# Eight products instead of seven in the first chunks of each feed-forward, with the combined inputs formed beside them

## The chip, the cores and the metric

The kernel runs on one core of one Trainium2 chip. The metric is the device time of one execution in microseconds (us). The engines are named as the profile names them: PE (TensorE; its weight loads are PEld), DVE (VectorE), ACT (ScalarE), POOL (GpSimd) and SP (SyncE, which only issues DMAs here).

## What is computed

One step of one hybrid decoder layer on 1024 prompt tokens and 64 sample tokens (1088 columns together), float32, model width 1024, feed-forward width 2816. The change touches only the two feed-forward parts, which stand before and after the mixing part:

```python
h = x + 0.5 * _swiglu(_rmsnorm(x, w['ffn1_norm']), w['ffn1_w1'], w['ffn1_w3'], w['ffn1_w2'])
...          # projection, windowed attention, recurrent heads, gates, w_out
y = h + 0.5 * _swiglu(_rmsnorm(h, w['ffn2_norm']), w['ffn2_w1'], w['ffn2_w3'], w['ffn2_w2'])

def _rmsnorm(x, g):
    y = xf * lax.rsqrt(jnp.mean(xf * xf, axis=-1, keepdims=True) + EPS)
    return y * g
def _swiglu(x, w1, w3, w2):
    return (jax.nn.silu(x @ w1) * (x @ w3)) @ w2
```

## The kernel before, in words

The residual stands transposed in SBUF: eight tiles `h[k]` of 128 features by 1088 tokens. Every float32 matrix product is made of three fp32r matmuls: each operand is split into a high part (ACT casts it to fp32r: `split`, L137) and a low part (the difference, on DVE or POOL: L138), and the products high·high, high·low and low·high are added in PSUM.

A feed-forward has two stages. **Stage A** (`stage_a`) makes silu(u·w1) times u·w3, where u is the normed residual, for 22 chunks of 128 of the 2816 features, and stores each chunk to DRAM (`p_d`). The second stage multiplies by w2. Stage A takes w1 and w3 of a chunk, the two halves of the 1024 input features and two pairs of token quarters (272 tokens each) as a 2x2 block product. That would be eight block products; the kernel computes seven (Strassen-Winograd, the table `PRODUCTS`). A block product is four matmul triples for each of two token groups `s`, so 24 matmuls of 272 columns, and a chunk has 168 of them. The weights are combined per chunk on POOL (`sums13`, L427) and split by `parts13`. The inputs are combined once per feed-forward, in `combine(s, kb, ...)` for s = 0, 1 and kb = 0 to 3:

- two POOL multiplications of 544 columns (h times the reciprocal root mean square, L303) and two DVE multiplications by the gain (L304) give the four normed quarters `q`;
- four DVE operations of 272 columns make the combinations `tt` (L306 to L309);
- two splits give seven slots of high and low parts, `U[s,"h"]` and `U[s,"l"]` (tiles u0h, u0l, u1h, u1l): ACT casts of 816 and 1088 columns, a POOL difference of 816 and a DVE difference of 1088.

In the first chunk the products run with s = 0 alone and then with s = 1 alone; all others take both. `combine(1, ...)` is deferred into that first chunk.

Ahead of the first feed-forward, `load_x` loads nine token tiles, squares them on ACT, transposes them on PE (L275), copies them into `h` (L278), takes the root (`rstd`, L216 to L222), spreads it over the partitions with matmuls (`spread`, L287 to L289) and calls `combine`, for tiles 0 to 4 and then for 5 to 8. Ahead of the second, the last product of the mixing part (`flush` over four ranges of 272 columns) updates `h` on DVE (L575), `norm_half(g, s, k)` squares `h` (L382, L385), sums on PE (L389) and calls `combine` for s = 0 after the second range and for s = 1 after the fourth.

The Python program sets the order of emission: functions are put off by `defer` against a clock of PE time and run from `tick` between matmuls, or by `force` at the latest. The framework's scheduler then orders each engine's queue, and every engine runs its queue strictly in order. Wait points are semaphores. PSUM has eight banks; in the first part of a stage they are handed out singly (`psum`), from `banks(False)` on in three pairs (`pair`).

Of the kernel before, what the change touches and what calls it, by code (L numbers as in the profile page):

```python
# [58 lines left out]
class Layer:  # L59
    def __init__(self, tc, ctx, io):  # L60
# [165 lines left out]
    def load_x(self, g, weights):  # L226
# [35 lines left out]
        group(rest)  # L262
        rb = self.spread([(0, 96, dgs[4][:, 32:P])] + [(96 + j * P, P, dgs[5 + j]) for j in range(3)]
                         + [(480, 32, dgs[8][:NS, 0:32]), (512, 32, dgs[8][:NS, 32:NS])])
        self.close("xl")
        self.open("ar", "right", "u1h", "u1l")
        for kb in range(4):
            self.defer(1.0 + 2.2 * kb, lambda kb=kb: self.combine(1, kb, g, rb), ("u", 1))

    def h_part(self, i, x, m, half):  # L270
# [1 line left out]
        ph = self.psum((P, 4, P))
        for c in range(4):
            k = half * 4 + c
            nc.tensor.transpose(ph[:, c, :m], x[:m, k * P:(k + 1) * P], self.ident[:m, :m])  # L275
        for c in range(4):
            k = half * 4 + c
            (nc.scalar.copy if half else nc.vector.tensor_copy)(out=self.h[k][:, i * P:i * P + m], in_=ph[:, c, :m])  # L278
# [1136 lines left out]
```

## Time and profile before

| | |
|---|---|
| median of 3 runs | 2487.96 us (2485.41 to 2488.25) |
| profiled execution | 2485.03 us, its span in the trace 2483.2 us |
| busy | PE 95%, DVE 55%, ACT 28%, POOL 18% |
| chain that ended last | PE 89%, DVE 6%, DMA 2%, ACT, POOL and issue 1% each |
| matmuls of stage A (L487) | 36% of that chain |

PE is busy nearly everywhere. The slices of the page in which it isn't are the first two of 40 and the 28th and 29th (62 us each): the start of the first feed-forward and the start of the second. A busy share is not a speed: the row PEclk is the clock that was granted to PE, and it is low in the same slices.

### The profile page before, as it was taken

The numbers are of one execution on the slowest core, as the hardware profiler recorded it, in microseconds if no ns is written. First come the engines' busy times: TensorE is split into PE (matmuls) and PEld (weight loads), VectorE is DVE, ScalarE is ACT, GpSimd is POOL, SyncE is SP. The second block draws the span as 40 slices with busy tenths as digits, with TensorE's granted clock in tenths as the row PEclk, the third lists the DMA queues.
The fourth block names the chain that finished last, engine by engine and source line by source line (L and its number), as shares of the span: only waits on it lengthen the run. The fifth ranks groups of instructions, "written<-read, shape, count | busy, mean of one in ns | idle before, by whom it ended". The sixth has DMA issues, their size and how long they took to land.

```text
span 2483.2 us, 40296 instructions
## 1 busy us (share of the span) xinstructions
PE 2363.5 (95%) x16635; PEld 2330.5 (94%) x16635; DVE 1354.3 (55%) x2348; ACT 703.8 (28%) x1299; POOL 443.3 (18%) x321
## 2 busy tenths in 40 slices
PE   2699999999999999999999999995899999999999
PEld 2699999999999899999999999994799999999999
DVE  6744444457676724440544447658644444467766
ACT  4322222232121523332222254323222222231211
POOL 4522222210000411111111100026322222200000
PEclk6799999999999999999999999996899999999999
DMA  3122222234233222112112285300122222242312
GB/s 107 58 80 74 73 76 74 75 119 162 74 106 74 84 72 68 56 62 77 48 56 67 81 265 162 94 4 11 58 79 79 79 79 79 79 143 103 105 38 73
DMA packets 226468, 207.97 MB, mean 84 GB/s; under 512 B 22835, under 2 KB 207956, under 8 KB 226268
## 3 DMA queue, kind: packets, MB, share of 16 engines
q1 hardware_dynamic: 215168, 195.79, 25.3%
q10 hardware_dynamic: 11116, 9.60, 1.2%
q8 instruction: 131, 2.15, 0.4%
q14 instruction: 53, 0.43, 0.1%
HBM read 152.20 MB, written 54.13 MB: 83 GB/s over the span
## 4 chain that ended last, share of the span: by engine, by line
PE 89%; DVE 6%; DMA 2%; ACT 1%; POOL 1%; issue 1%; ACTq 0%; SPq 0%; DVEq 0%; POOLq 0%
PE pp L487 36%; PE ps L199 15%; PE ps L201 15%; PE ps L200 15%; PE ps L1062 2%; PE ps L871 1%; DVE q L304 1%; PE ps L836 1%; DVE tt L308 1%; DVE tt L306 1%; DMA raw<-in_ffn_w 1%; PE ps L861 1%; DMA g<-gate_d 1%; DVE tt L307 0%; POOL q L303 0%
## 5 line engine op out<-in xcount | busy, mean ns | idle before, releaser
L575 DVE SCALAR_TENSOR_TENSOR h<-ps,h 128x384 f32<-128x384 f32 (+2 forms) x632 | 326.3, 529 | 192.8 <-PE ps L201 192.5
L487 PE MATMUL pp<-u1h,wah 128*128 128x272 f32 x1232 | 359.3, 293 | 21.4 <-ACT u1h L137 17.6
L487 PE MATMUL pp<-u1l,wah 128*128 128x272 f32 x1232 | 357.5, 290 | 15.7 <-POOL u1l L138 15.7
L487 PE MATMUL pp<-u0h,wah 128*128 128x272 f32 x1232 | 360.4, 292 | 2.9 <-DVE ep L492 1.3
L487 PE MATMUL pp<-u1h,wal 128*128 128x272 f32 x1232 | 358.6, 291 | 3.4 <-DVE wal L138 3.4
L487 PE MATMUL pp<-u0h,wal 128*128 128x272 f32 x1232 | 361.2, 293 | 0.0
L487 PE MATMUL pp<-u0l,wah 128*128 128x272 f32 x1232 | 360.1, 292 | 0.0
L199 PE MATMUL ps<-ph,wbh 128*128 128x384 f32 (+1 forms) x1056 | 346.3, 328 | 0.3 <-DVE ev L492 0.3
L201 PE MATMUL ps<-ph,wbl 128*128 128x384 f32 (+1 forms) x1056 | 344.9, 327 | 0.0
L200 PE MATMUL ps<-pl,wbh 128*128 128x384 f32 (+1 forms) x1056 | 344.7, 326 | 0.0
L199 PE MATMUL ps<-u,wah 128*128 128x384 f32 (+1 forms) x768 | 259.3, 338 | 0.0
L487 PEld LDWEIGHTS pp<-u1h,wah 128*128 128x128 f32 x1232 | 234.2, 191 | 24.4 <-ACT u1h L137 19.7
L201 PE MATMUL ps<-u,wal 128*128 128x384 f32 (+1 forms) x768 | 251.3, 327 | 0.0
L487 PEld LDWEIGHTS pp<-u1l,wah 128*128 128x128 f32 x1232 | 235.1, 191 | 17.2 <-POOL u1l L138 17.2
L200 PE MATMUL ps<-u,wah 128*128 128x384 f32 (+1 forms) x768 | 251.1, 327 | 0.0
L487 PEld LDWEIGHTS pp<-u0h,wah 128*128 128x128 f32 x1232 | 236.3, 192 | 4.3 <-DVE ep L492 2.4
L487 PEld LDWEIGHTS pp<-u1h,wal 128*128 128x128 f32 x1232 | 235.2, 191 | 4.1 <-DVE wal L138 4.1
L487 PEld LDWEIGHTS pp<-u0l,wah 128*128 128x128 f32 x1232 | 236.4, 192 | 0.0
L487 PEld LDWEIGHTS pp<-u0h,wal 128*128 128x128 f32 x1232 | 236.0, 192 | 0.0
L137 ACT CAST wah<-raw 128x1024 fp32r<-128x1024 f32 x134 | 140.8, 1050 | 272.7 <-issue 98.8
L137 ACT CAST wah<-sm 128x1024 fp32r<-128x1024 f32 x96 | 80.2, 835 | 447.2 <-PE pp L487 441.1
L199 PEld LDWEIGHTS ps<-ph,wbh 128*128 128x128 f32 x1056 | 198.8, 188 | 1.1 <-DVE ev L492 0.6
(324 smaller groups left out, 4318.4 us busy)
## 6 DMA issues: line engine op xcount, KB each, us to landing
raw<-in_ffn_w SPq DMA_DIRECT2D x132, 512.0 KB
pl<-p_d SPq DMA_DIRECT2D x44, 544.0 KB
p_d<-ep SPq DMA_DIRECT2D x80, 272.0 KB
raw<-in_w_in SPq DMA_DIRECT2D x34, 512.0 KB
gate_d<-gt SPq DMA_DIRECT2D x40, 192.0 KB
g<-gate_d SPq DMA_DIRECT2D x32, 192.0 KB
h_d<-h ACTq DMA_DIRECT2D x8, 544.0 KB
h<-h_d SPq DMA_DIRECT2D x8, 544.0 KB
```

The lines of the kernel that those rows point to most:

```text
L137: nc.scalar.copy(out=hi, in_=src)
L199: nc.tensor.matmul(out, lhsT=wh, rhs=uh, start=(i == 0), stop=False)
L200: nc.tensor.matmul(out, lhsT=wh, rhs=ul, start=False, stop=False)
L201: nc.tensor.matmul(out, lhsT=wl, rhs=uh, start=False, stop=(i == n - 1))
L304: nc.vector.tensor_scalar(out=q[:, 2 * j:2 * j + 2, :], in0=q[:, 2 * j:2 * j + 2, :], scalar1=g[:, k:k + 1], scalar2=None, op0=ALU.mult)
L306: nc.vector.tensor_tensor(out=tt[:, 1, :], in0=q[:, 2, :], in1=q[:, 0, :], op=ALU.subtract)
L308: nc.vector.tensor_tensor(out=tt[:, 2, :], in0=q[:, 1, :], in1=tt[:, 1, :], op=ALU.add)
L487: nc.tensor.matmul(out, lhsT=w[:, kw], rhs=u[:, slot, kb, :], start=(opens and kb == 0 and j == 0), stop=(kb == 3 and j == 2), skip_group_ ...
L575: nc.vector.scalar_tensor_tensor(out=self.h[k][:, sl], in0=po[:, :n], scalar=scale, in1=self.h[k][:, sl], op0=ALU.mult, op1=ALU.add)
L836: nc.tensor.matmul(pq[kv][:, i, :w], lhsT=self.q[c][hs, q0:q0 + P], rhs=self.kT[hs, k0:k0 + w], start=True, stop=True)
L861: nc.tensor.transpose(pp[:, c, :], sts[kv][0][:, c, j * P:(j + 1) * P], self.ident)
L1062: nc.tensor.matmul(pl[:, c], lhsT=ke[:, c, :], rhs=qv[:, c, :, 1, :], start=True, stop=True)
```

## The change

- The first three chunks of the first feed-forward and the first two of the second (`np_` = 3 and 2) are computed by a new function `plain` with eight products. They need only the four normed quarters, not the combinations. In chunk 0 the products go kb by kb, so that kb = 0 can start alone; in later plain chunks all of w1 comes before w3.
- The norm is `normed`: two DVE operations of 544 columns (`scalar_tensor_tensor`, h times gain times reciprocal root) in place of two on POOL and two on DVE. `quarters` splits the four quarters at once (ACT cast and DVE difference of 1088 columns each); POOL has no part in it.
- The combinations come later, in eight calls of `three` (4.0 us of PE time apart, from `mixed`), which norm again and form and split three slots; `fourth` forms the last one for all kb at once from the high and low parts, after the plain chunks. The slot numbers in `PRODUCTS` are renamed to match.
- Chunk 0 needs no `sums13`, and its weights are split once instead of twice over. Only chunk 0's weights are loaded before tiles 5 to 8.
- `load_x`: squares and transposes of tiles 5 to 8 are deferred into chunk 0; `h_part` transposes two tiles into one PSUM bank and copies 256 columns at a time, DVE one feature block of the bank and ACT the other.

The core of the diff:

```diff
+        ss = squares(range(0, 5))
+        for i in (0, 2, 4):
+            for k in range(0, KC, 2):
+                self.h_part(xt[i:i + 2] if i < 4 else xt[4:5], i * P, k)
+        diagonals(range(0, 5), ss)
         rb = self.spread([(i * P, P, dgs[i]) for i in range(4)] + [(512, 32, dgs[4][:, 0:32])])
         for kb in range(4):
-            self.combine(0, kb, g, rb)
...
+            self.quarters(0, kb, g, rb)
...
+        self.defer(1.0, rest, ("u", 1))
+        self.defer(4.5, norm, ("u", 1))
...
+    def normed(self, s, kb, g, rb):
...
+        for j in range(2):
+            k = kb + 4 * j
+            nc.vector.scalar_tensor_tensor(out=q[:, 2 * j:2 * j + 2, :].rearrange("p a n -> p (a n)"), in0=self.h[k][:, c0:c0 + 2 * QN], scalar=g[:, k:k + 1],
+                                           in1=rb[:, 0:2 * QN], op0=ALU.mult, op1=ALU.mult)
...
+        self.split(self.U[s, "h"][:, 0:4, kb, :], self.U[s, "l"][:, 0:4, kb, :], self.normed(s, kb, g, rb))
...
+            self.defer(2.0 + 4.0 * i, lambda s=s, kb=kb: self.three(s, kb, g, rbs[s]), "t")
+
+    def three(self, s, kb, g, rb):
+        nc = self.nc
+        q = self.normed(s, kb, g, rb)
         tt = self.t("e", [P, 4, QN], F32, 3, name="tt")
...
-            nc.gpsimd.tensor_tensor(out=q[:, 2 * j:2 * j + 2, :].rearrange("p a n -> p (a n)"), in0=self.h[k][:, c0:c0 + 2 * QN], in1=rb[:, 0:2 * QN], op=ALU.mult)
-            nc.vector.tensor_scalar(out=q[:, 2 * j:2 * j + 2, :], in0=q[:, 2 * j:2 * j + 2, :], scalar1=g[:, k:k + 1], scalar2=None, op0=ALU.mult)
...
+        nc.vector.tensor_tensor(out=tt[:, 0:2, :], in0=q[:, 1:3, :], in1=q[:, 0:1, :].to_broadcast([P, 2, QN]), op=ALU.subtract)
         nc.vector.tensor_tensor(out=tt[:, 2, :], in0=q[:, 1, :], in1=tt[:, 1, :], op=ALU.add)
...
-        self.split(uh[:, 0:3, kb, :], ul[:, 0:3, kb, :], q[:, 1:4, :], nc.gpsimd)
-        self.split(uh[:, 3:7, kb, :], ul[:, 3:7, kb, :], tt)
+        nc.vector.tensor_tensor(out=t4, in0=uh[:, 6].bitcast(F32), in1=uh[:, 3].bitcast(F32), op=ALU.subtract)
+        nc.vector.tensor_tensor(out=t4, in0=t4, in1=ul[:, 6].bitcast(F32), op=ALU.add)
+        nc.vector.tensor_tensor(out=t4, in0=t4, in1=ul[:, 3].bitcast(F32), op=ALU.subtract)
+        self.split(uh[:, 0], ul[:, 0], t4)
...
+    def plain(self, f, w, p_d, turns):
...
+            order = [(kb, j, x) for kb in range(4) for j in range(2) for x in range(2)]
+            if f:
+                order.sort(key=lambda o: o[2])
+            else:
+                self.force(("u", s))
...
+                for t in range(2):
+                    for i, (a, u) in enumerate(((wh, uh), (wh, ul), (wl, uh))):
+                        nc.tensor.matmul(ps[x][t][:, :QN], lhsT=a[:, k], rhs=u[:, 2 * j + t, kb, :], start=(k == 0 and i == 0), stop=(k == KC - 1 and i == 2),
+                                         skip_group_check=True)
...
+            for t in range(2):
+                a = ep[:, 2 * t + s, :]
+                nc.scalar.activation(out=a, in_=ps[0][t][:, :QN], func=AF.Silu)
+                nc.vector.scalar_tensor_tensor(out=a, in0=ps[1][t][:, :QN], scalar=-1.0, in1=a, op0=ALU.mult, op1=ALU.mult)
+            turns[s]()
...
+        self.force("t")
+        for s in range(2):
+            self.fourth(s)
+        self.banks(False)
```

**DVE's queue at the start of the second feed-forward, before.** `h` from a `ps` tile is an update by the last product of the mixing part; `q` and `tt` are those of `combine(0, kb)` above.

```order
L289 COPY rb_15922<-ps_15924 128x32
L575 SCALAR_TENSOR_TENSOR h_13949<-ps_15952,h_13949 128x272
L304 TENSOR_SCALAR q_15937<-q_15937,c_ffn_norm 128x544 x2
L307 TENSOR_TENSOR tt_15938<-q_15937 128x272
L306 TENSOR_TENSOR tt_15938<-q_15937 128x272
L575 SCALAR_TENSOR_TENSOR h_13950<-ps_15963,h_13950 128x272
L308 TENSOR_TENSOR tt_15938<-q_15937,tt_15938 128x272
L575 SCALAR_TENSOR_TENSOR h_13951<-ps_15973,h_13951 128x272
L309 TENSOR_TENSOR tt_15938<-tt_15938,q_15937 128x272
```

The same place in the changed kernel (L666 is the update of `h`, L319 the norm, L139 a low part):

```order
L309 COPY rb_15885<-ps_15887 128x32
L319 SCALAR_TENSOR_TENSOR q_15897<-h_13922,c_ffn_norm,rb_15885 128x544
L319 SCALAR_TENSOR_TENSOR q_15897<-h_13926,c_ffn_norm,rb_15885 128x544
L319 SCALAR_TENSOR_TENSOR q_15902<-h_13923,c_ffn_norm,rb_15885 128x544
L319 SCALAR_TENSOR_TENSOR q_15902<-h_13927,c_ffn_norm,rb_15885 128x544
L139 TENSOR_TENSOR u0l_15896<-q_15897,u0h_15895 128x4x272
L319 SCALAR_TENSOR_TENSOR q_15907<-h_13924,c_ffn_norm,rb_15885 128x544
L139 TENSOR_TENSOR u0l_15896<-q_15902,u0h_15895 128x4x272
L319 SCALAR_TENSOR_TENSOR q_15907<-h_13928,c_ffn_norm,rb_15885 128x544
L319 SCALAR_TENSOR_TENSOR q_15912<-h_13925,c_ffn_norm,rb_15885 128x544
L319 SCALAR_TENSOR_TENSOR q_15912<-h_13929,c_ffn_norm,rb_15885 128x544
L139 TENSOR_TENSOR u0l_15896<-q_15907,u0h_15895 128x4x272
```

The updates of the fourth range of `h`, which before stood between the pieces of all four `combine` calls, now stand behind three of the four quarters; behind the fourth comes the rest of them.

**PE's queue in chunk 0 of the first feed-forward, changed.** L503 is a matmul of `plain`, L295 a transpose of token tiles 5 and 6.

```order
L307 MATMUL ps_237<-dx_233,ones 128x32
L503 MATMUL ps_279<-u0h_245,wah_112 128x272
L503 MATMUL ps_280<-u0h_245,wah_112 128x272
L503 MATMUL ps_281<-u0h_245,wah_116 128x272
L295 MATMUL ps_302<-ident,x_120 128x128
L295 MATMUL ps_302<-ident,x_122 128x128
```

Before, the transposes of tiles 5 to 8 came right behind `spread` and ahead of every product. Now all 32 of them lie among the first 39 matmuls of chunk 0, and the last matmuls of the second `spread` 36 matmuls before the end of s = 0 (of 96).

**DVE's queue at the first seven-product chunk of the second feed-forward, changed.** L348 to L350 are `fourth` for s = 0 (t_2299) and s = 1 (t_2300), L586 takes a product out of PSUM.

```order
L139 TENSOR_TENSOR u1l_16107<-tt_16507,u1h_16106 128x3x272
L349 TENSOR_TENSOR t_2299_16594<-t_2299_16594,u0l_15896 128x1088
L348 TENSOR_TENSOR t_2300_16600<-u1h_16106 128x1088
L350 TENSOR_TENSOR t_2299_16594<-t_2299_16594,u0l_15896 128x1088
L349 TENSOR_TENSOR t_2300_16600<-t_2300_16600,u1l_16107 128x1088
L139 TENSOR_TENSOR wal_16639<-raw_16193,wah_16638 128x1024
L139 TENSOR_TENSOR u0l_15896<-t_2299_16594,u0h_15895 128x1088
L350 TENSOR_TENSOR t_2300_16600<-t_2300_16600,u1l_16107 128x1088
L586 TENSOR_TENSOR ev_16610<-ev_16610,pp_16642 128x544
L139 TENSOR_TENSOR wal_16694<-sm_16467,wah_16693 128x512
L139 TENSOR_TENSOR u1l_16107<-t_2300_16600,u1h_16106 128x1088
L586 TENSOR_TENSOR ep_16611<-ev_16610,pp_16703 128x544
```

The first row is the last of the eight `three` calls; the two L586 rows, which free PSUM pairs for PE, stand behind seven operations of 1024 or 1088 columns.

## Rows read from the trace of the kernel before

**Rows 1.** The page: busy time of the engines, and the span in 40 slices of 62 us (tenths of busy time; granted PE clock in tenths).

```profile
PE 2363.5 (95%) x16635; PEld 2330.5 (94%) x16635; DVE 1354.3 (55%) x2348; ACT 703.8 (28%) x1299; POOL 443.3 (18%) x321
PE   2699999999999999999999999995899999999999
PEclk6799999999999999999999999996899999999999
```

**Rows 2.** Busy time by stretches at the start of the first feed-forward (stretch, length, busy us and instructions of each engine, granted PE clock, DMA share, GB/s).

```profile
30.00:65.00 35.00, 6.94 (x40) 6.32 (x38) 31.93 (x57) 10.93 (x28) 21.07 (x12) 0.55 0.06 14
65.00:80.00 15.00, 10.50 (x62) 9.94 (x61) 12.22 (x19) 7.86 (x10) 10.38 (x6) 0.82 0.11 34
80.00:115.00 35.00, 20.41 (x100) 18.17 (x101) 27.91 (x32) 10.99 (x15) 18.39 (x11) 0.66 0.13 38
115.00:140.00 25.00, 25.00 (x201) 25.00 (x201) 14.83 (x17) 7.03 (x10) 9.47 (x7) 1.00 0.28 83
```

**Rows 3.** The same at the start of the second feed-forward.

```profile
1640.00:1670.00 30.00, 29.77 (x228) 29.32 (x226) 18.75 (x43) 9.97 (x15) 8.44 (x6) 1.00 0.00 1
1670.00:1690.00 20.00, 10.94 (x68) 10.41 (x68) 18.45 (x27) 6.96 (x10) 14.80 (x9) 0.79 0.00 1
1690.00:1710.00 20.00, 10.41 (x47) 10.33 (x48) 16.29 (x27) 6.83 (x11) 12.53 (x8) 0.50 0.00 1
1710.00:1730.00 20.00, 11.09 (x67) 10.34 (x67) 13.18 (x15) 5.70 (x7) 9.09 (x7) 0.76 0.00 0
1730.00:1755.00 25.00, 10.13 (x39) 7.66 (x37) 22.33 (x26) 7.14 (x8) 15.86 (x9) 0.57 0.18 53
```

**Rows 4.** ACT in order of time, line 494 alone: the copy of a chunk's first product out of PSUM, once per pass. The 128x544 rows are whole chunks: chunks 2 and 3 of the first feed-forward, then 1 and 2 of the second.

```profile
140.41 0.61 ACT L494 COPY ev<-pp 128x544 f32<-128x544 f32 x1 [1.49 <-PE pp L487]
161.50 0.61 ACT L494 COPY ev<-pp 128x544 f32<-128x544 f32 x1 [1.49 <-PE pp L487]
...
1768.45 0.61 ACT L494 COPY ev<-pp 128x544 f32<-128x544 f32 x1 [0.46 <-PE pp L487]
1789.55 0.61 ACT L494 COPY ev<-pp 128x544 f32<-128x544 f32 x1 [1.49 <-PE pp L487]
```

**Rows 5.** All engines in order of time at the first norm: root, spread, POOL's norm, DVE.

```profile
25.27 0.18 DVE L218 RECIPROCAL xr<-xr 128x5 f32<-128x5 f32 x1
26.63 2.34 PE L287 MATMUL ps<-dx,ones 128*128 128x128 f32 x10 [12.12 <-DVE dx L256]
28.74 0.59 ACT L288 COPY rb<-ps 128x512 f32<-128x512 f32 x1 [0.32 <-PE ps L287]
29.40 5.63 POOL L303 TENSOR_TENSOR q<-h,rb 128x544 f32<-128x544 f32 x4 [5.21 <-ACT rb L288]
33.76 1.57 DVE L307 TENSOR_TENSOR tt<-q 128x272 f32<-128x272 f32 x1
39.06 0.43 DVE L307 TENSOR_TENSOR tt<-q 128x272 f32<-128x272 f32 x1
39.41 0.43 DVE L306 TENSOR_TENSOR tt<-q 128x272 f32<-128x272 f32 x1
```

**Rows 6.** Groups of instructions by line and shape (count | busy us, mean ns of one | idle before, and on whom).

```profile
L492 DVE TENSOR_TENSOR ep<-ev,pp 128x544 f32<-128x544 f32 x80 | 57.7, 722 | 160.5 <-PE pp L487 160.5
L138 DVE TENSOR_TENSOR pl<-pl,ph 128x1088 fp32r<-128x1088 f32 x44 | 56.6, 1286 | 1.0 <-ACT ph L137 0.2
L137 ACT CAST ph<-pl 128x1088 fp32r<-128x1088 f32 x44 | 48.6, 1104 | 178.3 <-PE ps L200 150.1 <-DMA pl<-p_d 28.2
L138 DVE TENSOR_TENSOR wal<-raw,wah 128x1024 fp32r<-128x1024 f32 x100 | 125.5, 1255 | 32.1 <-ACT wah L137 32.1
L304 DVE TENSOR_SCALAR q<-q,c_ffn_norm 128x544 f32<-128x544 f32 x32 | 29.8, 962 | 8.0 <-POOL q L303 8.0
L306 DVE TENSOR_TENSOR tt<-q 128x272 f32<-128x272 f32 x16 | 17.2, 1078 | 0.1
```

**Rows 7.** PE alone by stretches (length, busy us and matmuls, granted clock, DMA share, GB/s): the 32 transposes of tiles 5 to 8, and the first matmuls of chunk 0.

```profile
28.00:30.00 2.00, 2.00 (x12) 0.50 0.00 0
30.00:32.00 2.00, 2.00 (x11) 0.50 0.00 0
32.00:34.00 2.00, 2.00 (x19) 0.79 0.00 0
34.00:36.00 2.00, 0.60 (x6) 1.00 0.00 0
66.00:68.00 2.00, 2.00 (x10) 0.50 0.83 254
68.00:70.00 2.00, 2.00 (x11) 0.50 0.00 0
70.00:72.00 2.00, 2.00 (x16) 0.90 0.00 0
```

**Rows 8.** PE in order of time, two matmuls of chunk 0 at the low clock.

```profile
66.26 0.43 PE L487 MATMUL pp<-u0h,wal 128*128 128x272 f32 x1
66.48 0.43 PE L487 MATMUL pp<-u0h,wah 128*128 128x272 f32 x1
```

**Rows 9.** DVE and ACT in order of time at the start of the second feed-forward: the last update of the second range of `h`, the first root and the copy of its spread, the first and last update of the fourth range, the second root.

```profile
1661.52 0.44 DVE L575 SCALAR_TENSOR_TENSOR h<-ps,h 128x272 f32<-128x272 f32 x1 [1.43 <-PE ps L201]
1666.29 0.17 DVE L216 TENSOR_SCALAR mv<-ps 128x5 f32<-128x5 f32 x1 [0.95 <-PE ps L389]
1671.42 0.59 ACT L288 COPY rb<-ps 128x512 f32<-128x512 f32 x1 [4.73 <-PE ps L287]
1672.40 0.44 DVE L575 SCALAR_TENSOR_TENSOR h<-ps,h 128x272 f32<-128x272 f32 x1 [0.64 <-PE ps L201]
1699.61 0.43 DVE L575 SCALAR_TENSOR_TENSOR h<-ps,h 128x272 f32<-128x272 f32 x1
1706.35 0.16 DVE L216 TENSOR_SCALAR mv<-ps 128x5 f32<-128x5 f32 x1 [3.57 <-PE ps L389]
1709.85 0.48 DVE L395 TENSOR_SCALAR dg<-ident,mr 128x128 f32<-128x128 f32 x2
1715.77 0.58 ACT L288 COPY rb<-ps 128x512 f32<-128x512 f32 x1
```

More of the change, by code (lines that the diff above doesn't have):

```diff
@@ L240, in load_x, with squares @@
                 weights()
-        first, rest = range(0, 5), range(5, 9)
         dgs = {}
-        def group(tiles):
+        def squares(tiles):
             ss = self.t("ss", [P, 5], F32, 2)
@@ L250, in group, with diagonals @@
                 nc.scalar.activation(out=jk[:m], in_=x[:m], func=AF.Square, accum_out=ss[:m, j:j + 1])
-                for half in range(2):
-                    self.h_part(i, x, m, half)
+            return ss
+        def diagonals(tiles, ss):
             rr = self.rstd(ss, [P, 5], 1.0 / D, "x")
@@ L262, in load_x @@
[L262 to L270, printed above, removed]
-        nc = self.nc
[L272 to L278, printed above, removed]
+            self.quarters(0, kb, g, rb)
@@ new lines, in rest, with norm @@
+        def rest():
+            ss = squares(range(5, 9))
+            for i in (5, 7):
+                for k in range(0, KC, 2):
+                    self.h_part(xt[i:i + 2], i * P, k)
+            diagonals(range(5, 9), ss)
+        def norm():
+            rb2 = self.spread([(0, 96, dgs[4][:, 32:P])] + [(96 + j * P, P, dgs[5 + j]) for j in range(3)]
+                              + [(480, 32, dgs[8][:NS, 0:32]), (512, 32, dgs[8][:NS, 32:NS])])
+            self.close("xl")
+            self.open("ar", "right", "u1h", "u1l")
+            for kb in range(4):
+                self.quarters(1, kb, g, rb2)
+            self.mixed(g, (rb, rb2))
@@ new lines, in load_x, with h_part @@
+        self.defer(1.0, rest, ("u", 1))
+        self.defer(4.5, norm, ("u", 1))
+    def h_part(self, xs, c0, k0):
+        nc = self.nc
+        n = sum(m for _, m in xs)
+        ph = self.psum((P, 2, 2 * P))
+        for c in range(2):
+            o = 0
+            for x, m in xs:
+                nc.tensor.transpose(ph[:, c, o:o + m], x[:m, (k0 + c) * P:(k0 + c + 1) * P], self.ident[:m, :m])
+                o += m
+        for c in range(2):
+            (nc.scalar.copy if c else nc.vector.tensor_copy)(out=self.h[k0 + c][:, c0:c0 + n], in_=ph[:, c, :n])
@@ L403, in apply @@
             for kb in range(4):
[L404 removed]
+                self.quarters(s, kb, g, rb)
+            self.rbs[s] = rb
+            if s:
+                self.mixed(g, self.rbs)
         self.defer(SUM_U, sums, key)
@@ L509, in stage_a, with ffn @@
                     tt(c2, c2, v, ALU.mult)
-            dst = p_d[f].rearrange("p (s two n) -> p two s n", s=2, two=2)
-            src = e2.rearrange("p (two s) n -> p two s n", two=2)
-            for two in range(2):
-                nc.sync.dma_start(out=dst[:, two, sl], in_=src[:, two, sl])
+            self.to_dram(p_d[f], e2, sl)
             for un in range(4):
                 parts.pop((q, un))
-    def ffn(self, w1, w3, w2_, begun, after, late, between=None):
+    def ffn(self, w1, w3, w2_, begun, np_, after, late, between=None):
         nc = self.nc
```

83 lines of the change are left out of this document (56 added, 27 removed).

## The prediction

> **What bounds the kernel now.** I read the page first: PE is busy 95% of the span, and its row of slices falls only in the first two and in the 28th and 29th, where the granted clock falls too [rows 1]. So all that this change can win lies in two places, the starts of the two feed-forwards; elsewhere PE runs through. Then the stretches. At the first start PE is busy 6.9 of the 35 us from 30 to 65 and 20.4 of the 35 from 80 to 115, at a granted clock of 0.55 and 0.66 of the full one, while DVE is busy 31.9 and 27.9 [rows 2]; only from 115 does PE run through at 1.00. At the second start PE runs through until 1670, and from there to 1755 DVE is busy 70 of 85 us, PE 43, at clocks between 0.50 and 0.79 [rows 3]. There the forming of the seven combined inputs on DVE and POOL ends last.
>
> Why DVE is slow there: a 272-column operation takes 0.43 us alone, but 1.57 while POOL's norm is running; POOL's group of four holds from 29.40 to 35.03 [rows 5]. Over the kernel L306 comes to 1.08 in the mean and L304 to 0.96 [rows 6].
>
> As a ruler I use the copy of a chunk's first product. Once a stage runs freely these copies are 21.09 us apart (140.41 and 161.50 in the first feed-forward, 1768.45 and 1789.55 in the second) [rows 4]. What comes behind such a copy is the same in both kernels, so the copy of the first seven-product chunk tells the gain: chunk 3 at 161.50, and chunk 2 of the second feed-forward at 1789.55.
>
> **Prices.** A chunk of 168 matmuls is 21.09 us, so a matmul is 0.1255 and the eighth product (24 of them) 3.0; five plain chunks cost 15.1 us of PE, and a plain chunk lasts 24.1. At the lower clock (1.2 GHz, granted 0.50) matmuls start 0.22 to 0.23 apart [rows 8], which I take as 0.23. The trace shows no norm operation of the new kind (544 columns, two tensors and a column of gains). From below it is bounded by half of L304's mean, about 0.48, from above by twice the 272-column update of L575, 0.87 [rows 9]; I take the 0.72 of the two-tensor operation of the same 544 columns, which is nearest [rows 6]. ACT's cast of 1088 columns is 1.10, DVE's difference 1.29 (816 columns, between 0.72 and 1.29: 1.0), a weight difference 1.25 [rows 6]. So `quarters` is 2.7 us of DVE per kb, `three` 1.44 + 0.72 + 0.43 + 1.0 = 3.6 (28.7 for all eight), `fourth` 4 x 1.29 for each s (10.3). I use whole durations, though DVE starts 0.43 us operations 0.35 apart [rows 5]: that is my reserve for semaphores.
>
> **First feed-forward.** The second weight combination isn't needed any more, so its cast (1.05 for 1024 columns, by the 1.10 for 1088) and difference (1.25) no longer stand ahead of the root: the spread root, ready at 29.3 [rows 5], comes at 27.0. DVE's queue has five norm operations, then two low parts: the first low part is ready at 27.2 + 3.6 + 1.3 = 32.1, the others at 33.4, 37.3 and 39.0 (a norm, a cast and a PSUM copy lie between). ACT has a square and a weight cast ahead of the first high part, about 1.1 each, so that is ready at 27.0 + 2.2 + 1.1 = 30.3, and PE starts chunk 0 at 31, where before it began at 65.6. It mixes 96 matmuls with 32 transposes (some 0.2 each by the counts of [rows 7]). There the granted clock was still 0.50 at 32 and at 70, with PE busy from 28 and from 66; as the work here is broken up, I take it as low until 40. By then 19 matmuls and 20 transposes are done; 77 matmuls, 12 transposes and a spread at the full clock (9.7 + 1.8 + 1.2) end s = 0 at 53.
>
> The second norm hangs on the transposes, the last of them 20 matmuls after 40, at 44.3. A copy, a weight difference and the root take DVE to 48.1 (0.4 + 1.25 + 2.1: from reciprocal to spread it was 1.4 [rows 5], and there is more before and behind), spread and copy go to 50.0; six norm operations, then low parts at 56.2, 57.5, 58.8. The fourth stands behind two norms of its own and the first pieces of `three` and comes at 65.6. PE waits 3 us behind s = 0, does three groups of 24 matmuls as they come, and ends chunk 0 at 65.6 + 3.0 = 68.7.
>
> Chunk 1 needs w3's low part 6 us later, at 74.7; in DVE's queue it stands behind pieces of `three` and the evictions, and I get 76.9: 2.2 lost. Chunks 1 and 2 then end at 68.7 + 48.2 + 2.2 = 119.1. DVE has 37 us of `three`, `fourth`, evictions and weights to do in the 42 up to there, so it keeps pace. The first product takes 3.2 with its copy, and I allow 1.2 for the last plain results to leave PSUM before pairs can be opened: 123.5 against 161.5. **Gain 38.0.**
>
> A rule on the new copies. In the trace DVE or ACT empties a bank alone; now each bank is shared by both. The Trainium skill, page "PSUM — Partial Sum Buffer", section "PSUM bank collisions raise a hardware error", says that two engines must not touch one bank's same partitions at once, reads included, so ACT's half waits for DVE's. By it each of the two groups ends one copy later than with both at once, some 0.4 us at the price of L575's 272 columns; without it the sum would be 0.4 to 0.9 us lower. I leave both out, since the first is covered by the weight splits.
>
> **Second feed-forward.** The spread root is ready at 1672.0 [rows 9], as before. Before, updates of `h`'s fourth range stood between `combine`'s pieces and went from 1672.40 to 1699.61, and with them the squares: the second root started at 1706.35 and its copy at 1715.77 [rows 9]. Now they stand behind eight norm operations and three low parts (5.8 + 3.9): the first is done at 1682.1, the last, with PE refilling banks at the low clock, at 1687.5. PE can write some five of the eight groups meanwhile, then stands about 6 us: what is late next is this last range. From the last update to the root I take the 4.3 of the undisturbed first half (1661.96 to 1666.29), from there to the finished copy its 5.7 (to 1672.0) [rows 9]: root at 1691.8, copy at 1697.4, 18.9 earlier than before. Low parts of s = 1 follow at 1701.6, 1703.6, 1707.0, 1709.0. PE has s = 0 of chunk 0 meanwhile: 1687.5 to 1702, 5 us of it at the low clock. s = 1 takes 12 more and waits for nothing: 1714.1. Chunk 1, whose w3 low part is there at 1720.7 instead of 1720.1, ends at 1738.8.
>
> Here DVE has no slack: the queue behind that w3 part adds up to 24.5, so the last `three` ends at 1745.2, just when the second product needs its slot (1744 to 1746). Behind it seven operations of `fourth` and weights and two evictions, 12.9 together, come before the second of these evictions, at 1758.1, which the sixth product waits for; PE would start that at 1755.3: 2.8 lost. The ruler's copy is at 1738.8 + 1.5 for the pairs + 3.2 = 1743.5, and with the 2.8 behind it the gain is 1789.55 - 1746.3. **Gain 43.2.**
>
> **Sum.** 2485.0 - 38.0 - 43.2 = 2403.8, so **2404**. The profiled execution lies 2.9 under the median of the runs shown, so 2407 fits that; I keep 2404, as the reserve above is on the safe side. If every norm cost 0.87, the chains would grow by about 3 in each start and DVE's lateness by some 5 more: 2419. With 0.48, 0.35-spacing and no wait for w3: 2388.
>
> **Rivals.**
> 1. DVE is late with the combinations. It has 39 us of `three` and `fourth` per feed-forward between evictions that PE waits for. At 1.4 times the price that is 15.6 more each, 5 of it hidden in the first: 2404 + 26 = 2430. For it: the 1.57 and the mean of 1.08 for a 0.43 operation [rows 5, 6]. Against: POOL keeps only the weight sums in these chunks, its norm and low parts are gone. Chance 0.12.
> 2. PE's clock stays at 1.2 GHz through chunk 0 of the first feed-forward, because transposes and short waits break its work up. Then 173 matmuls cost 0.1 more each: 2421. Before, from 80 to 100, broken-up matmuls had such clocks (0.66 over 80 to 115) [rows 2]. Against: 32 transposes in a row took the clock from 0.50 to 1.00 [rows 7]. The Trainium skill, page "TensorE: Matmul & The Clock Gate", section "Part 4: PE-mode transpose", says that transposes do not count as PE's activity and the full clock does not engage for them; by it this rival would be the likely case. This trace disagrees (0.50, 0.50, 0.79, 1.00 over the transposes). Chance 0.06.
> 3. Slower. Rival 1 at full price: if DVE's operations in the plain chunks were held up as L306 was (2.5 times), `three` and `fourth` would take 98 us instead of 39 in each feed-forward, PE would stand before the first seven-product chunk, and the time be 2404 + 59 + 54 = 2517. It turns into a loss from a factor of 2.1 on, as 41 us per start is then lost. Only steady POOL work beside DVE would do that, and the queue has none. Chance 0.02.
> 4. The eighth products eat what the starts give, because PE waits for something else, such as weights: the start has less DMA traffic ahead of it than before, so I give 0.02, at 2485.
>
> **How the numbers follow.** Forecast 0.78 (2388 to 2419). The range 2386 to 2428 takes in the bounds, rival 2 and most of rival 1. A measurement of this kernel can tell 0.2% (5 us) from no change: faster 0.97, same 0.01, slower 0.02.
>
> **What would show it.** PE's first product near 31, not 65; the ruler's copy of chunk 3 at 123.5, and from then 21.09 apart; in the second start the last update of `h` near 1649.5 (38 earlier than 1687.5) and the ruler's copy of chunk 2 near 1705; no DVE 272-column operation over 1 us except beside weight sums. I am wrong if PE stands long before the first seven-product chunk (rival 1), if the clock is 0.50 beyond 45 (rival 2), or if updates of `h` still trickle over 25 us.

## The result and the profile after

The changed kernel takes **2411.79 us** (median of 4 runs, 2410.3 to 2414.58) against 2488.11 beside it (4 runs, 2485.41 to 2489.32): ratio 0.9696, 95% interval 0.9679 to 0.9713, 76 us faster. The profiled execution took 2412.2, its span is 2410.1. The forecast was 2404 in a range of 2386 to 2428.

Line numbers from here on are the changed kernel's: the ruler's copy is L588 (L494 before), the norm L319, `three` L340 and L341, `fourth` L348 to L350, low parts L139, plain products L503 with their silu L509 and DVE eviction L510, the updates of `h` L666, POOL's weight sums L469, the single-column sums of squares L428.

The page, as [rows 1]:

```profile
PE 2367.3 (98%) x16755; PEld 2336.5 (97%) x16755; DVE 1325.9 (55%) x2317; ACT 688.3 (29%) x1268; POOL 336.4 (14%) x253
PE   6999999999999999999999999999999999999999
PEclk8999999999999999999999999998999999999999
```

The hole of the 28th and 29th slice is gone; one slice at a lower clock is left. The stretches of the first start, as [rows 2], and of the second, as [rows 3] but 41 us earlier (stretch, length, busy us and instructions of PE, PEld, DVE, ACT and POOL, granted clock, DMA share, GB/s):

```profile
30.00:65.00 35.00, 33.76 (x237) 30.87 (x235) 30.38 (x58) 14.83 (x23) 0.00 (x0) 0.95 0.22 61
65.00:80.00 15.00, 14.68 (x117) 14.68 (x118) 14.97 (x23) 5.21 (x8) 0.00 (x0) 1.00 0.35 108
80.00:115.00 35.00, 35.00 (x281) 35.00 (x280) 31.06 (x33) 11.44 (x17) 14.00 (x7) 1.00 0.11 37
...
1630.00:1640.00 10.00, 5.20 (x43) 4.98 (x41) 9.45 (x13) 4.86 (x5) 0.00 (x0) 0.88 0.01 2
1640.00:1650.00 10.00, 8.79 (x37) 8.27 (x38) 4.19 (x10) 4.72 (x9) 5.24 (x4) 0.50 0.00 0
1650.00:1660.00 10.00, 10.00 (x46) 10.00 (x47) 1.06 (x7) 0.21 (x1) 0.00 (x0) 0.50 0.00 0
1660.00:1670.00 10.00, 10.00 (x78) 10.00 (x77) 7.72 (x14) 2.79 (x3) 0.00 (x0) 0.93 0.01 2
1670.00:1700.00 30.00, 30.00 (x242) 30.00 (x240) 29.76 (x34) 10.17 (x13) 13.28 (x7) 1.00 0.06 20
1700.00:1710.00 10.00, 5.56 (x45) 5.34 (x43) 9.97 (x15) 5.05 (x9) 0.00 (x0) 0.96 0.00 1
1710.00:1720.00 10.00, 9.14 (x54) 9.17 (x55) 9.97 (x15) 2.49 (x4) 0.00 (x0) 0.70 0.34 110
```

The first start is as good as closed: from 30 to 115 PE is busy 83.4 of 85 us. The second has two holes: a clock of 0.50 from 1640 to 1660, where PE is busy and DVE works 5.3 of the 20 us, and at 1700 to 1720 a stand of PE, and a clock of 0.70 behind it, while DVE is full. The ruler (ACT in order of time; the copies of the two spread roots of the second start among them), as [rows 4] and the root copies of [rows 9]:

```profile
116.26 0.61 ACT L588 COPY ev<-pp 128x544 f32<-128x544 f32 x1 [2.01 <-PE pp L581]
137.35 0.61 ACT L588 COPY ev<-pp 128x544 f32<-128x544 f32 x1 [1.49 <-PE pp L581]
...
1630.32 0.59 ACT L308 COPY rb<-ps 128x512 f32<-128x512 f32 x1 [4.72 <-PE ps L307]
1662.90 0.59 ACT L308 COPY rb<-ps 128x512 f32<-128x512 f32 x1 [3.99 <-PE ps L307]
1716.61 0.61 ACT L588 COPY ev<-pp 128x544 f32<-128x544 f32 x1 [2.14 <-DMA p_d<-ep]
1737.61 0.61 ACT L588 COPY ev<-pp 128x544 f32<-128x544 f32 x1 [1.44 <-PE pp L581]
```

116.26 and 1716.61 are the copies that were at 161.50 and 1789.55 in [rows 4]; 1630.32 was 1671.42 in [rows 9]. So the first feed-forward gained 45.2 us (38.0 forecast). At the second norm 41.1 of it was left: 4.1 went on the way. The second start gained 118.13 - 86.29 = 31.8 (43.2 forecast). At the end 73 us stand.

**What PE did at the low clock** (PE in order of time, the four groups of sums of the second half's squares, each of ten 128x1 matmuls, with plain products between; then the first step of the second root, on DVE):

```profile
1644.33 2.29 PE L428 MATMUL ps<-ones,sq 128*128 128x1 f32 x10 [0.61 <-POOL sq L424]
1648.44 2.13 PE L428 MATMUL ps<-ones,sq 128*128 128x1 f32 x10
1652.39 2.13 PE L428 MATMUL ps<-ones,sq 128*128 128x1 f32 x10
1656.33 2.13 PE L428 MATMUL ps<-ones,sq 128*128 128x1 f32 x10
...
1658.50 0.17 DVE L217 TENSOR_SCALAR mv<-ps 128x5 f32<-128x5 f32 x1 [14.31 <-PE ps L428]
```

PE had stood 5.4 us for `h` until 1640.6, the clock had fallen to 0.50 (1638 to 1640), and with these groups in between it stayed there until 1661. The second root, which needs the last group, started at 1658.50; DVE had waited 14.3 us for that group. PE itself did not wait for the root: from 1641 until the end of chunk 1 at 1705.5 it stood 0.6 us in all. What it lost there it lost by its own speed. In the first half of the same norm such groups stood between twelve products each and the clock was 1.00 throughout (1616 to 1628), so the groups alone did not bring it down; here they followed a stand.

**Why DVE was late at 1705** (DVE, POOL, ACT and PE, each in order of time):

```profile
1696.44 1.81 DVE L319 SCALAR_TENSOR_TENSOR q<-h,c_ffn_norm,rb 128x544 f32<-128x544 f32 x1
1698.28 1.69 DVE L340 TENSOR_TENSOR tt<-q 128x544 f32<-128x544 f32 x1
1704.11 0.77 DVE L319 SCALAR_TENSOR_TENSOR q<-h,c_ffn_norm,rb 128x544 f32<-128x544 f32 x1
1705.97 0.72 DVE L340 TENSOR_TENSOR tt<-q 128x544 f32<-128x544 f32 x1
1709.94 0.78 DVE L510 SCALAR_TENSOR_TENSOR ep<-ps,ep 128x272 f32<-128x272 f32 x2
...
1696.29 1.37 POOL L469 TENSOR_TENSOR sm<-sm,raw 128x512 f32<-128x512 f32 x1
1697.63 1.77 POOL L469 TENSOR_TENSOR raw<-raw 128x512 f32<-128x512 f32 x1
...
1707.64 0.40 ACT L509 ACTIVATE ep<-ps 128x272 f32<-128x272 f32 x1 [0.56 <-DVE u1l L139]
...
1710.86 0.57 PE L581 MATMUL pp<-u0h,wah 128*128 128x272 f32 x1 [5.30 <-DVE ep L510]
```

The same two operations cost 1.8 and 1.7 us beside POOL's weight sums and 0.77 and 0.72 after them. PE finished chunk 1 at 1705.5 and stood 5.3 us for the eviction L510, which frees the PSUM banks. The Trainium skill, page "SBUF — State Buffer", section "SBUF: two separate sides", says that a DVE operation with two SBUF inputs and a POOL operation that reads SBUF exclude each other for the whole instruction; the rows agree in kind: from 1689 to 1699 one sum and one slowed operation come in turn, about 1.7 us to the pair, and 1.81 is 0.77 and 1.04 more. The two alone, 0.77 and 1.37, would add to 2.1, so that they shut each other out for the whole of their recorded times isn't shown.

### The profile page after: what moved, and what is told of

It reads as the page before. It is cut to its first block, busy times and chain, and to the rows that moved or that the text cites. A ratio compares the mean times of both kernels' runs of the same rounds, so it can differ in the third digit from the quotient of the medians.

```text
span 2410.1 us, 40328 instructions
## 1 busy us (share of the span) xinstructions
PE 2367.3 (98%) x16755; PEld 2336.5 (97%) x16755; DVE 1325.9 (55%) x2317; ACT 688.3 (29%) x1268; POOL 336.4 (14%) x253
## 4 chain that ended last, share of the span: by engine, by line
PE 91%; DVE 5%; DMA 2%; ACT 1%; issue 1%; POOL 0%; ACTq 0%; SPq 0%; DVEq 0%; POOLq 0%
PE pp L581 34%; PE ps L200 15%; PE ps L202 15%; PE ps L201 15%; PE ps L503 3%; PE ps L1153 2%; DVE q L319 1%; PE ps L962 1%; DMA g<-gate_d 1%; PE ps L927 1%; PE ps L952 1%; DMA raw<-in_ffn_w 1%; PE ps L428 1%; DVE u0l L139 0%; DVE u1l L139 0%
## 5 line engine op out<-in xcount | busy, mean ns | idle before, releaser
L666 DVE SCALAR_TENSOR_TENSOR h<-ps,h 128x384 f32<-128x384 f32 (+2 forms) x632 | 325.1, 528 | 193.8 <-PE ps L202 193.5
L581 PE MATMUL pp<-u0h,wah 128*128 128x272 f32 x1092 | 315.5, 289 | 6.6 <-DVE ep L510 5.3
L581 PE MATMUL pp<-u0h,wal 128*128 128x272 f32 x1092 | 317.3, 291 | 0.0
L581 PE MATMUL pp<-u0l,wah 128*128 128x272 f32 x1092 | 316.2, 290 | 0.0
L581 PE MATMUL pp<-u1h,wah 128*128 128x272 f32 x1092 | 315.6, 289 | 0.0
L581 PE MATMUL pp<-u1h,wal 128*128 128x272 f32 x1092 | 315.0, 288 | 0.0
L581 PE MATMUL pp<-u1l,wah 128*128 128x272 f32 x1092 | 313.3, 287 | 0.0
L581 PEld LDWEIGHTS pp<-u0h,wah 128*128 128x128 f32 x1092 | 206.2, 189 | 7.3 <-ACT wah L138 5.5
L581 PEld LDWEIGHTS pp<-u0l,wah 128*128 128x128 f32 x1092 | 206.3, 189 | 0.0
L581 PEld LDWEIGHTS pp<-u0h,wal 128*128 128x128 f32 x1092 | 206.1, 189 | 0.0
L201 PEld LDWEIGHTS ps<-pl,wbh 128*128 128x128 f32 x1056 | 199.1, 189 | 0.0
```

The source lines that it names most:

```text
L201: nc.tensor.matmul(out, lhsT=wh, rhs=ul, start=False, stop=False)
L581: nc.tensor.matmul(out, lhsT=w[:, kw], rhs=u[:, slot, kb, :], start=(opens and kb == 0 and j == 0), stop=(kb == 3 and j == 2), skip_group_ ...
L666: nc.vector.scalar_tensor_tensor(out=self.h[k][:, sl], in0=po[:, :n], scalar=scale, in1=self.h[k][:, sl], op0=ALU.mult, op1=ALU.add)
```

## The experiments

Each was timed against the kernel before on the same chip. Beside the times I give three lengths from each trace: the ruler of chunk 3 in the first feed-forward ("start 1"), the time from there to the first spread root's copy of the second feed-forward ("between"), and from that to the ruler of its chunk 3, from which on the copies are within 0.1 us of 21.09 apart in every kernel ("start 2"). "The theory held" means that the result fits the theory of the expectation and not its rival.

| kernel | median us (range) | ratio, 95% interval | start 1 | between | start 2 |
|---|---|---|---|---|---|
| before | 2488.11 | | 161.50 | 1509.9 | 139.2 |
| the change | 2411.79 (2410.3 to 2414.6) | 0.9679 to 0.9713 | 116.26 | 1514.1 | 107.3 |
| 1 sums together | 2407.05 (2405.1 to 2409.8) | 0.9653 to 0.9686 | 115.95 | 1514.5 | 104.9 |
| 2 in place | 2413.20 (2411.2 to 2415.1) | 0.9682 to 0.9711 | 118.29 | 1510.0 | 108.6 |
| 3 weight sums on DVE | 2407.96 (2406.0 to 2409.6) | 0.9661 to 0.9690 | 115.94 | 1512.2 | 104.5 |
| 4 three plain chunks | 2408.60 (2405.6 to 2410.6) | 0.9663 to 0.9692 | 115.42 | 1514.1 | 103.8 |
| 5 norm alone | 2452.67 (2448.1 to 2455.3) | 0.9824 to 0.9867 | 142.47 | 1517.0 | 121.0 |
| 6 norm on POOL | 2455.70 (2455.0 to 2458.8) | 0.9849 to 0.9883 | 135.68 | 1514.9 | 130.1 |
| 7 old copies | 2417.96 (2415.5 to 2419.1) | 0.9694 to 0.9727 | 119.30 | 1516.3 | 107.9 |
| 8 one group of sums | 2408.74 (2400.1 to 2411.3) | 0.9645 to 0.9693 | 116.03 | 1511.0 | 98.2 |
| 9 = 8 and 3 | 2401.55 (2399.6 to 2404.9) | 0.9644 to 0.9675 | 115.84 | 1515.1 | 96.5 |
| 10 = 9, both halves | 2407.80 (2400.7 to 2409.5) | 0.9658 to 0.9697 | 116.41 | 1518.4 | 98.0 |
| 11 two plain chunks | 2418.55 (2417.1 to 2419.2) | 0.9711 to 0.9743 | 121.25 | 1513.4 | 107.6 |

How much such a length scatters can be read from kernels that are alike in it: start 1 is 115.4 to 116.4 in seven kernels (the change, 1, 3, 4, 8, 9, 10), start 2 is 107.3 to 107.9 in three (the change, 7, 11), but "between" runs from 1509.9 to 1517.0 in kernels with the same lines there. The times carry that scatter. Only the intervals of 5 and 6, which lie above that of the change, and of 9, which lies below it, are clear of it; those of the others overlap with it. For these the two starts tell more than the median, each from one execution.

**1. Sums together.** The theory: the sums in between hold the clock down, and POOL's weight sums make DVE late; these are two losses.

```diff
-        self.defer(SUM_U, sums, key)
+        held = self.held = [sums] if k == 1 else self.held + [sums]
+        if not s:
+            self.defer(SUM_U, sums, key)
+        elif k == KC - 1:
+            self.defer(6.0, lambda: [f() for f in held], key)
         if k == KC - 1:
-            self.defer(SUM_U + 0.1, root, key)
+            self.defer(6.1 if s else SUM_U + 0.1, root, key)
```

> The changed kernel, with the four groups of single-column sums of the second half put together, some 6 us of matmuls behind the last update, instead of one group after every 9 plain matmuls. Theory: the groups in between keep PE's granted clock at 0.50 from 1640 to 1661; together they let it come back to 1.00 by about 1650, and DVE's lateness in chunk 1 then eats most of it: second spread root 1 to 4 us earlier than 1662.9, first copy of chunk 2 some 3 us earlier than 1716.6, time about 2409 against 2412. Rival (the gap of 5.4 us alone put the clock down and it comes back by itself at about 1660): clock 0.50 until 1660, time within 1.5 us of 2412.

Measured 2407.05, and the clock does two things in one trace (stretches as above, then the forty sums):

```profile
1641.00:1644.00 3.00, 3.00 (x16) 3.00 (x15) 3.00 (x8) 2.17 (x5) 0.93 (x1) 0.50 0.00 0
1644.00:1649.00 5.00, 5.00 (x41) 5.00 (x40) 0.33 (x1) 2.22 (x5) 4.37 (x4) 0.96 0.00 0
1649.00:1652.00 3.00, 3.00 (x26) 3.00 (x26) 0.00 (x0) 0.00 (x0) 0.00 (x0) 0.87 0.00 0
1652.00:1655.00 3.00, 3.00 (x15) 3.00 (x16) 0.00 (x0) 0.00 (x0) 0.00 (x0) 0.50 0.03 5
1655.00:1660.00 5.00, 5.00 (x23) 5.00 (x24) 2.10 (x11) 0.21 (x1) 0.00 (x0) 0.50 0.00 0
...
1648.94 6.45 PE L428 MATMUL ps<-ones,sq 128*128 128x1 f32 x40
```

It comes back at 1644 over unbroken matmuls, and falls again while the forty single-column matmuls run, though the trace shows PE busy all the time: no stand of PE put it down there. That speaks against the rival. The program's order on PE changed too (chunk 0's first products went ahead of the last updates, which split the 5.4 us gap into several of about 1), so this run alone doesn't divide its gain between gap and sums. The second root's copy came 30.96 behind the first instead of 32.58, and start 2 is 2.4 shorter. Chunk 1 ended 71.7 us after the first root's copy instead of 75.2; from there to the ruler it took 1.2 longer, as PE still stood for DVE.

**8. One group of sums.** DVE, idle there, adds the squares up first:

```diff
         nc.gpsimd.tensor_tensor(out=sq, in0=sq, in1=self.sq[:, 0, :], op=ALU.add)
+        if s and k > 1:
+            nc.vector.tensor_tensor(out=sq, in0=sq, in1=self.acc, op=ALU.add)
+        self.acc = sq
...
-        self.defer(SUM_U, sums, key)
+        if not s or k == KC - 1:
+            self.defer(6.0 if s else SUM_U, sums, key)
```

> The changed kernel, with the squares of the second half added up on DVE first (three operations of 544 columns), so that one group of ten single-column matmuls is left instead of four. Theory (these groups hold the clock down): granted clock at 1.00 from about 1645 on, with no second fall in 1650 to 1660 as the four groups put together have it; second spread root at about 1658 instead of 1662.9; then DVE sets the end: time about 2406, and 2407 with the four groups together. Rival (the rise at 1644 came from the shorter gaps ahead of it, not from the sums): clock 0.50 over most of 1645 to 1660 and time 2410 to 2412.

In the trace the second fall is gone:

```profile
1640.00:1645.00 5.00, 5.00 (x40) 5.00 (x39) 3.45 (x5) 2.77 (x6) 5.00 (x4) 0.94 0.00 0
1645.00:1650.00 5.00, 4.04 (x34) 3.83 (x32) 3.08 (x10) 0.21 (x1) 0.39 (x1) 1.00 0.00 0
1650.00:1655.00 5.00, 3.81 (x32) 3.58 (x31) 4.04 (x10) 1.91 (x3) 0.00 (x0) 1.00 0.02 5
...
1646.86 1.28 PE L431 MATMUL ps<-ones,sq 128*128 128x1 f32 x10 [0.96 <-DVE sq L426]
```

The second root's copy follows the first by 24.3 us, and start 2 is 9.1 shorter than in the change. In 1 the plain products and the last updates stand in the same order on PE, so 8 against 1 is the cleaner comparison: 6.7 us of start 2. Not all of that is clock, as the thirty sums that are gone would have taken 3.8 us of PE even at the full clock: ten cost 1.28 there, and 2.13 at the low one. The time is less clear than the trace: the profiled execution took 2400.1, the other three, of which there is no trace, 2407 to 2411. That the clock stays up with fewer sums is shown; what it is worth in the median isn't settled by this run (9 has it again).

**2. In place.** Three single differences in the norm's buffer instead of a second buffer.

> The changed kernel, with the combinations formed in the norm's own buffer (three 272-column operations instead of one of 544 and one of 272), so that one buffer a piece is needed instead of two. Theory (DVE's work itself is late in chunk 1 of the second feed-forward): the silu's wait for a buffer goes, but PE still stands over 4 us before the first seven-product chunk; time 2411 to 2414. Rival (the shared buffers make the wait): PE's wait of 5.3 us goes, time about 2407.

Measured 2413.20, PE still stands 5.4 us there (3.5 for a weight's low part, L139, and 1.9 for ACT's copy, L588): the shared buffer did not make the wait, and the theory held. The extra DVE operation shows in start 1, 2.0 longer.

**3. Weight sums on DVE.** `sums13` of the second feed-forward's first seven-product chunk with `nc.vector` in place of `nc.gpsimd`.

> The changed kernel, with the four weight sums of the second feed-forward's first seven-product chunk on DVE (some 0.65 us each) instead of POOL. Theory: POOL's sums of 1685.9 to 1699.4 slow DVE's norm from 0.72 to 1.8 us each and cost about 7 us of DVE; without them DVE is 4 us less late, PE's wait of 5.3 us falls to about 1, time about 2408. Rival (DVE's own load makes the late operations slow): norms stay at 1.5 us and more, the four sums come on top, time about 2415.

Measured 2407.96. The groups (lines and shapes, 1670 to 1712; first this kernel, then the change):

```profile
L319 DVE SCALAR_TENSOR_TENSOR q<-h,c_ffn_norm,rb 128x544 f32<-128x544 f32 x17 | 13.8, 818 | 0.1
L340 DVE TENSOR_TENSOR tt<-q 128x544 f32<-128x544 f32 x8 | 5.7, 717 | 0.0
L469 DVE TENSOR_TENSOR sm<-raw,raw 128x512 f32<-128x512 f32 x1 | 0.7, 684 | 0.0
```

```profile
L319 DVE SCALAR_TENSOR_TENSOR q<-h,c_ffn_norm,rb 128x544 f32<-128x544 f32 x19 | 18.4, 994 | 0.1
L340 DVE TENSOR_TENSOR tt<-q 128x544 f32<-128x544 f32 x7 | 7.0, 995 | 0.1
```

L340 is back at its undisturbed 0.72; four sums of 0.68 cost DVE less than POOL's blocking did, and PE's waits in the first seven-product chunk fell from 5.3 to 3.5 us, 2.5 of it for a weight's low part on DVE and not for banks; the expectation had about 1. In kind the theory held: start 2 is 2.8 shorter.

**4. Three plain chunks** in the second feed-forward (2 became 3 in its call).

> The changed kernel with three plain chunks in the second feed-forward too, instead of two. The eighth product costs PE 3.0 us more. Theory (PE loses 5.3 us by waiting and some 2 us by the lower clock behind it because DVE isn't ready at the end of chunk 1; one chunk later it is): time about 2408 to 2409. Rival (DVE is still late a chunk later, or the wait was never DVE's load): the 3.0 us come on top, time about 2415.

Measured 2408.60: the eighth product's 3.0 us bought back more than it cost, as PE no longer stands ahead of the seven-product chunks (no wait over 0.6 us after 1641). The theory held: start 2 is 3.5 shorter.

**5 and 6: the parts of the change.** 5 is the kernel before with L303 and L304 as one DVE operation and the low parts on DVE; 6 is the change with only the norm undone; its low parts stay on DVE (6's edit, lines shortened):

```diff
-            nc.vector.scalar_tensor_tensor(out=q..., in0=self.h[k]..., scalar=g[:, k:k + 1], in1=rb..., op0=ALU.mult, op1=ALU.mult)
+            nc.gpsimd.tensor_tensor(out=q..., in0=self.h[k]..., in1=rb..., op=ALU.mult)
+            nc.vector.tensor_scalar(out=q..., in0=q..., scalar1=g[:, k:k + 1], scalar2=None, op0=ALU.mult)
```

> The kernel before, with one part of the change alone: the norm (one scalar_tensor_tensor instead of a product on POOL and a scaling on DVE) and the three low parts on DVE. Seven products from the first chunk on, old copies. Theory (DVE held up by POOL was the larger part of the old starts): per kb DVE then has 1.44 + 1.72 + 0.99 + 1.28, some 5.4 us, 22 for each half; the first start ends some 28 us earlier and the second some 20: time about 2440, between 2430 and 2452. Rival (what counts is that PE has eight products to do meanwhile; the norm alone gives under 15 us): 2472 or more.

> The changed kernel, with the norm's product on POOL and its scaling on DVE again, as before. Theory (POOL's products hold DVE up): quarters cost DVE some 6 us more for each half and the pieces of three some 25 more in each feed-forward, of which 4 to 8 lie beside other work: time about 2460, between 2440 and 2480. Rival (eight products give the DVE time enough either way): under 2425.

Measured 2452.67 and 2455.70: both theories held in kind, 5 just past the slow end of its range. Each of the two brings under half of the gain. In start 1 they add up, though the low parts are in both: the norm alone brings 161.5 - 142.5 = 19.0, all but the norm 25.8, the whole change 45.2. In start 2 it is 18.2 and 9.1, both 31.9, so there one helps the other: in 6 PE stood 15.2 us before the first seven-product chunk, where it stands 5.3 in the change. My 28 for the norm in start 1 was too much, and the trace of 5 shows why (PE):

```profile
55.16 2.64 PE L287 MATMUL ps<-dx,ones 128*128 128x128 f32 x10 [20.05 <-DVE dx L256]
```

The second spread, ahead of every product in PE's queue, still waits 20.0 us (28.1 before) for diagonals that DVE makes behind the combinations of s = 0, and the first product starts at 58.2 (65.7 before, 28.8 in the change). So a part of the 25.8 is the new order, in which tiles 5 to 8 come within chunk 0; no run has that order without the eighth products, and what each is worth stays open.

**7. Old copies.**

> The changed kernel with the old copies of the transposes (128 columns each, DVE for the first four blocks of a tile and ACT for the other four). Theory (the wider copies are the small part): 1 to 4 us more, time 2412 to 2416. Rival (they carry the first norm's earlier start): over 6 us more, 2418 or above.

Measured 2417.96, by the median 6.2 more, at the edge of the rival (over 6, 2418 or above); beside the kernel before on the same chip it is less (ratio 0.9711 against 0.9696, intervals overlapping). The traces put only 3.0 of it into start 1, where the copies are; 2.2 lie in between and 0.6 in start 2, where no line differs. So the copies are worth about 3, and the rest I can't lay to them.

**9, 10 and 11.**

> The changed kernel with two of the edits together: squares of the second half added up on DVE, so that one group of single-column matmuls is left, and the first weight sums of the second feed-forward on DVE. Theory (two separate losses, the clock and DVE's lateness): the gains add up, the first copy of chunk 2 follows the first spread root of that feed-forward by 73 to 75 us instead of 86.3, time about 2401, between 2397 and 2405. Rival (both shorten the same wait): no better than the better of the two, 2407 to 2409.

Measured 2401.55: the theory held. The two gains nearly add up: start 2 is 96.5 against 107.3, 10.8 less, where the single ones are 9.1 and 2.8. (By the first copy itself it is 77.6, outside the 73 to 75 expected; that copy was late, as the next came 18.9 behind it.) Its interval lies below that of the change, so this version beats both kernels: by the medians 10 us under the change (timed at another time), 84 under the kernel before beside it.

> As the run before, with the squares of the first half added up on DVE as well, where PE runs through and each group costs it some 1.3 us at the full clock. Theory: 3 groups less, 3.8 us of PE: about 2397 to 2400. Rival (the later first root holds the DVE chain of this start up by as much): the same as the run before within 2 us.

Measured 2407.80, by the median worse than either case, though one of the four runs took 2400.7 and the interval overlaps with that of 9. Start 2 grew by 1.5, and the first root came 3.3 later than in 9 ("between", within its scatter): over both halves PE waited 4.2 us for DVE's added squares and 1.6 for the roots' diagonals (in the change 0.6 for POOL's squares and nothing for diagonals), and the clock was 0.75 and 0.56 in 1620 to 1630 and 1630 to 1640 (1.00 in 9). I take it that the matmuls saved were cheaper than that; the time alone doesn't show it.

> The changed kernel with two plain chunks in the first feed-forward, as in the second, instead of three: PE saves 3.0 us of eighth products. Theory (DVE needs the third chunk: its last combination of three kb ends at about 94 and the two fourths take some 12 more beside POOL's sums, while chunk 1 ends at about 92): PE stands some 10 us ahead of chunk 2; time about 2419, 2416 to 2424. Rival (DVE has slack there): about 2409.

Measured 2418.55: the theory held in the time. Before chunk 2 PE stood 4.7 us, not 10, but lost 3.4 more by clock (0.83 from 90 to 110); the ruler came 5.0 later.

## Why the prediction was right, and where its sizes were off

- **What bounds** was right: all of the gain came from the two starts, and 5 and 6 show that it needs both the norm's DVE operation and the rest of the change (eight products and their order).
- **Prices.** The norm operation, taken as 0.72, took 0.72 each in a row of four undisturbed and 0.77 to 0.78 alone; the 816-column difference 1.00, as taken. The slow end of 2419 is not quite the sum of its terms: 3 in each start and 5 make 2415, and only 5 in each start as well gives 2420.
- **First start, 38.0 forecast, 45.2 measured.** The order of events was right, the terms too long. PE began at 28.8 (31 forecast). The clock was back at 1.00 by 34, not 40, with transposes among the matmuls; rival 2 did not come, against the rule that stood beside it. The two copies out of one shared bank did run one behind the other (DVE's from 35.26 for 0.41, ACT's from 35.70). The second root's copy was done at 46.3 (50.0), the fourth low part at 61.4 (65.6), w3's at 75.2 (76.9).
- **Second start, 43.2 forecast, 31.8 measured.** Two terms failed. "5 us of it at the low clock" was 20, and "the 4.3 of the undisturbed first half" from the last update to the root was 14.3. The last update of `h` was even earlier than forecast (1644.2 against 1646.4, that is 1687.5 less the 41.1 by which this start came earlier), but root (1658.5) and chunk 1's end (1705.5) came 7.8 later. I had not seen that the second half's sums of squares stand between plain products, behind a stand of PE; with one group at the full clock the way from update to root was 7.3 (experiment 8). And "2.8 lost" behind the first product was a stand of 5.3 before it, and then a clock of 0.70, because beside POOL's seven weight sums, in 1686 to 1699, seven operations of DVE took about 1 us more each; from chunk 1's end to the ruler's copy it was 11.1, not 7.5, that is 3.6 us more than forecast. I had these sums in the text (as the one exception to the 272-column price) and gave them no time. That is rival 1 in small; experiment 3 took four of these sums away from POOL and got 2.8 us of start 2 back.
- **Between, 0 forecast, 4.1 lost.** Same lines in both kernels, at a lower clock in two places: the bias rows (first row of each) and the start of the mixing part; first before, then after.

```profile
579.00:599.00 20.00, 20.00 (x96) 17.37 (x96) 13.30 (x21) 6.21 (x9) 0.00 (x0) 0.91 0.69 243
840.00:860.00 20.00, 16.70 (x116) 15.21 (x114) 16.05 (x43) 9.79 (x34) 9.41 (x9) 0.91 0.43 161
```

```profile
535.00:555.00 20.00, 20.00 (x78) 15.79 (x77) 11.49 (x18) 6.39 (x9) 0.00 (x0) 0.74 0.68 240
796.00:816.00 20.00, 16.01 (x106) 14.90 (x106) 15.22 (x35) 10.23 (x33) 10.58 (x11) 0.83 0.35 140
```

That is 20 x 0.17 + 20 x 0.08 = 5.0 us by the clock. In 2, with the same lines as the change there, the two stretches (538 to 558, 798 to 818) had 0.91 and 0.91 and nothing was lost between; in 5 it was 7.1. So it looks like scatter of single executions; no experiment was aimed at it.

The two errors of size went in opposite directions, +7 and -11, and with the 4 between make the 8 us by which the trace misses 2404. That they partly cancelled is luck: without the 7 to spare in the first start the same trace would have been 2419, at the slow end of the bounds.

## What to carry to other kernels

When an edit gives PE work in a place where it used to stand, look at what else stands in its queue there: narrow sums are little work by their columns, but here, behind a stand of PE, the clock stayed at half for 20 us with them in between, and both PE's own work and the second root came 7.8 us later than forecast. And count the POOL operations that are left, not those that are removed: each that ran beside a DVE operation with two SBUF inputs cost DVE about 1 us here. Where DVE was late here, taking sums off POOL helped (2.8 us of start 2), and freeing a buffer did not.
